# The running sum of an encoder layer's output: from SBUF with VectorE's adds to DRAM with accumulating transfers

## The chip, the cores and the metric

One core of one Trainium2 chip runs the kernel. The metric is the device time of one execution in microseconds (us), the median of several runs.

## What is computed

One encoder layer on x of 512 tokens by 2048 features, in float32. A mixing stage (two head groups, a gated unit and a long convolution) ends in a projection that is added to x. Then comes the feed-forward layer, which this case is about, and a last normalization:

```python
h = rms_norm(x, norm2_g[l])
gv = h @ ffn_w_up[l]                                  # 2048 -> 2 * 5504
g = dwconv3(gv[..., :D_FF], ffn_dw_w[l], ffn_dw_b[l]) # three taps along the tokens
val = gv[..., D_FF:]
x = x + (jax.nn.gelu(g, approximate=False) * val) @ ffn_w_down[l]
...
return rms_norm(x, final_g)
```

## The kernel before

Every large matmul works on pairs: a float32 operand is split into a high part that TensorE takes exactly and the rest, and three matmuls (line 222, `mm3`) make one product. For weights ScalarE casts the high part and VectorE subtracts it from the raw tile (`exact_pair`, lines 143 and 144). Raw tiles of 512 KB come in SP's order from a plan (lines 88 to 125): `raw` with three buffers for w_in, w_out and w_up, `sraw` with four for w_down; cast and subtract run up to three units ahead of TensorE (`next_unit`, line 203). A scheduler of the framework orders each engine's instructions; each engine and SP then run theirs strictly in that order.

The feed-forward layer runs over 11 groups of up to 512 of the 5504 inner features. A group has 8 units of the gate's projection and 8 of the value's (`regular`, 24 matmuls each), with ScalarE, VectorE and GpSimd convolving and gating between (`conv_piece`, whose multiply by GpSimd is line 1113; `value_out`; `operands`). The multiplication by w_down of groups 0 to 9 is done for blocks of two by two with seven products (`strassen`, units 0 to 6, for each of two halves `dp` of the output columns: 14 units of 12 matmuls a group). These units stand between the projection units of the group after (`ffn_order`, lines 95 to 107); for the last of the ten groups products 3 to 6 of the second half follow the last projection without others between. Product u runs into a chain of two PSUM banks (tp = 0 and 1); a chain is read out after each product that ends in it, and some are then added to further.

The running sum x lies in SBUF, in `xacc` (32 KB of each partition). At the start of the layer `turn_x` turns it so that tokens lie on the partitions. After each product `down_out` has VectorE add the two banks to their place in it (`add_to`, line 1192). Product 3 belongs to three blocks; it is summed over the groups in `shared` (line 1201) and added three times at the end. For `next_unit` such work waits in `posts`, for `piece` in `pieces`.

The 11th group (384 features) takes no products of that kind: its w_down comes in eight tiles of 512 or 256 KB (units "L"), and 144 matmuls make sixteen blocks of 128 tokens by 512 columns; `last_out` adds a block to x, squares it and multiplies it by final_g (`grow`), `leave` scales it and stores it. First come the blocks of tokens 0 to 255, tile by tile as the weights come, then the others. Lines 1253 to 1350 hold this end.

Of the kernel before, what the change touches and what calls it, by code (L numbers as in the profile page):

```python
# [12 lines left out]
F32 = mybir.dt.float32  # L13
F32R = mybir.dt.float32r
AF = mybir.ActivationFunctionType
ALU = mybir.AluOpType

P = 128
D = 2048
# [32 lines left out]
def encoder_kernel(ctx: ExitStack, tc: tile.TileContext, a: dict, out: bass.AP):  # L52
# [783 lines left out]
    kp = pool("keep", side="right", stack=keep)  # L836
    xacc = kp.tile([P, KD, L], F32, name="xacc")
    ds_ = ExitStack()
# [16 lines left out]
    def done_a(q, ps):  # L855
        for f, o in enumerate(ps):
            ACT.copy(xacc[:, 4 * q + f, :], o)

# [140 lines left out]
    def done_b(q, ps):  # L999
        ts_ = []  # L1000
        for f, o in enumerate(ps):
            t = bo.tile([P, L], F32, tag="ev", name="tb", bufs=4)
            DVE.tensor_tensor(t, o, rbs[0], ALU.mult)
            ts_.append(t)
        for f, t in enumerate(ts_):
            x_ = xacc[:, 4 * q + f, :]
            POOL.tensor_tensor(t, t, res[q][:, f, :], ALU.add)
            DVE.tensor_tensor(x_, x_, t, ALU.add)
# [9 lines left out]
    def norm2(q):  # L1018
        H, Lo = h2[q]
        if q == 0:  # L1020
            ss2s.append(const.tile([P, L], F32, tag="acc", name="ss2", bufs=1))
        ss2 = ss2s[0]
        for f in range(4):
            k = 4 * q + f
            split_scaled(H[:, f, :], Lo[:, f, :], xacc[:, k, :], col("norm2", k))
            sq = (bo if q < 3 else A3).tile([P, L], F32, tag="ev", name="sq2", bufs=4 if q < 3 else 2)
            square_into(ss2, xacc[:, k, :], sq, k == 0)

# [37 lines left out]

    shared = ff.tile([P, 2, 2, 512], F32, name="shared")
    special["raw"] = lambda: ff.tile([P, 2, 512], F32, tag="sraw", name="sraw", bufs=4)
# [15 lines left out]

    def out_tile(t, q):

        return xacc[:, 4 * q : 4 * q + 4, t * P : (t + 1) * P]

    def as_out(ap):
        return ap.rearrange("p (k c) -> p k c", k=4)  # L1090

    def turn_x(k):

        o = sbank("xt")
        for t in range(NT):
            PE.transpose(o[:, t * P : (t + 1) * P], xacc[:, k, t * P : (t + 1) * P], ident)
        ACT.copy(xacc[:, k, :], o)

# [16 lines left out]
    def gate_out(gi):  # L1115
        gg[gi] = ff.tile([P, 4, L], F32, tag="gg", name="gg", bufs=1)
        for f, o in enumerate(ps_of.pop(("gate", gi))):
            DVE.tensor_tensor(gg[gi][:, f, :], o, r2[0], ALU.mult)
            pieces.append(lambda f=f: conv_piece(gi, f))
# [69 lines left out]

    def add_to(t, q, src):  # L1190
        x_ = out_tile(t, q)
        DVE.tensor_tensor(x_, x_, src, ALU.add)

    def down_out(gi, dp, u, tp):
        o = chains[dp, CHAIN[u]][tp]
        if u == 3:
            sh = shared[:, tp, dp, :]
            if gi == 0:
                ACT.copy(sh, o)
            else:  # L1200
                DVE.tensor_tensor(sh, sh, o, ALU.add)
            if gi == last - 1:
                for t, q in ((tp, dp + 2), (tp + 2, dp), (tp + 2, dp + 2)):
                    pieces.append(lambda t=t, q=q: add_to(t, q, as_out(sh)))
        else:
            t, q = ((tp, dp), (tp + 2, dp + 2), (tp, dp + 2), None, (tp + 2, dp + 2), (tp, dp), (tp + 2, dp))[u]
            add_to(t, q, as_out(o))

    def strassen(e):
# [9 lines left out]
        for tp in range(2):  # L1219
            ts_ = slice(tp * P, (tp + 1) * P)  # L1220
            for k in range(2):
                mm3(
                    chains[dp, CHAIN[u]][tp], H[:, u, k, ts_], Lo[:, u, k, ts_], hi[:, k, :], lo[:, k, :],
                    k == 0 and u not in (2, 3, 6), k == 1, True,
                )
            posts.append(lambda tp=tp: down_out(gi, dp, u, tp))

# [44 lines left out]
    def last_operands():  # L1272
        g = gg.pop(last)
        for f in range(nf):
            exact_pair(aH[:, f, :], aL[:, f, :], g[:, f, :])
        grow.append(ff.tile([P, D], F32, tag="gg", name="grow", bufs=1))
        SP.dma_start(grow[0], a["final_g"].partition_broadcast(P))

    grow, fin = [], {}
    for e in units:  # L1280
        if e[0] == "L":
# [6 lines left out]
    def last_out(t, q):  # L1288

        if q == 0:  # L1290
            if t < 2:
                w = ff.tile([P, D], F32, tag=("aH", "aL")[t], name="fin", bufs=1)
                fin[t] = [w[:, i * 512 : (i + 1) * 512] for i in range(4)]
            else:
                ws = [special["raw"]() for _ in range(2)]
                fin[t] = [ws[i // 2][:, i % 2, :] for i in range(4)]
        o = ps_of.pop(("last", t, q))
        x_ = fin[t][q]
        DVE.tensor_tensor(as_out(x_), out_tile(t, q), as_out(o), ALU.add)
        ACT.activation(tmp[q % 2], x_, AF.Square, accum_out=ssf[:, t, q : q + 1])  # L1300
# [10 lines left out]
    def leave(t):  # L1311
# [12 lines left out]
        for q in (0, 1, 3, 2):  # L1324
            SP.dma_start(out[t * P : (t + 1) * P, q * 512 : (q + 1) * 512], fin[t][q])

    for q in range(4):
        for k0 in range(0, nf, 2):
# [105 lines left out]
```

## Time and profile before

| | us |
|---|---|
| median of 3 runs (2086.36 to 2088.26) | 2087.02 |
| the profiled execution, its own time | 2086.55 |
| its span in the profile | 2084.7 |
| TensorE (PE) busy | 2059.8 |
| VectorE (DVE) busy | 1374.5 |
| ScalarE (ACT) busy | 758.6 |
| GpSimd (POOL) busy | 215.4 |
| bytes moved by DMA, mean over the span | 228.33 MB, 110 GB/s |

Busy times of the engines lie beside each other, so they don't add up to the span. A matmul of 512 columns is listed with some 390 ns, but matmuls are pipelined and start closer together than that. An engine's idle time is listed with what ended it. SP and the other queues that issue transfers are not counted as busy; a transfer's time to landing is listed with its issue. The DMA share is the mean busy share of the core's 16 DMA engines.

### The profile page before, as it was taken

To read this page: it belongs to the slowest core of one execution; us is meant where nothing else is said; L and a number is where in the kernel's file an instruction comes from. 1 tells how busy PE (TensorE), PEld (TensorE's weight loads), DVE (VectorE), ACT (ScalarE), POOL (GpSimd) and SP (SyncE) were. 2 spreads that over 40 slices of the span, in tenths; PEclk is the share of its full clock that TensorE was granted. 3 is DMA by queue.
4 is the path that set the end of the run, shared out by engine and by line. 5 is a ranking of instruction groups with operands and counts; after the bars stand their busy time and mean duration, and the time that the engine had idled before them with its cause. 6 is when DMAs were issued, how large, how long until landed. Compare 5 with 4: busy or idle time off the path is not lost.

```text
span 2084.7 us, 23478 instructions
## 1 busy us (share of the span) xinstructions
PE 2059.8 (99%) x9374; PEld 1706.9 (82%) x9374; DVE 1374.5 (66%) x1654; ACT 758.6 (36%) x954; POOL 215.4 (10%) x124
## 2 busy tenths in 40 slices
PE   8999999999999999999999999999999999999997
PEld 6888887888888888888888888888888888888886
DVE  6873565556897944755757666676755757666768
ACT  6433542222544442332333332333322333332334
POOL 0330211000003610100101001010100101001000
PEclk9999999999999999999999999999999999999999
DMA  8434233243323532332333333333332333333223
GB/s 298 137 116 141 81 91 91 81 141 105 108 82 121 172 91 82 100 113 90 111 97 104 103 101 102 91 101 102 101 113 90 111 97 103 105 101 94 91 84 136
DMA packets 112697, 228.33 MB, mean 110 GB/s; under 512 B 7147, under 2 KB 14507, under 8 KB 110668
## 3 DMA queue, kind: packets, MB, share of 16 engines
q1 hardware_dynamic: 107248, 216.74, 33.3%
q10 hardware_dynamic: 5340, 10.10, 1.4%
q8 instruction: 73, 1.20, 0.2%
q14 instruction: 36, 0.29, 0.0%
HBM read 218.42 MB, written 8.39 MB: 109 GB/s over the span
## 4 chain that ended last, share of the span: by engine, by line
PE 90%; DVE 7%; ACT 1%; issue 1%; DMA 1%; POOL 0%; ACTq 0%; SPq 0%; POOLq 0%; DVEq 0%
PE pa L226 19%; PE pa L224 19%; PE pa L225 19%; PE po L224 2%; PE po L226 2%; PE po L225 2%; PE se L225 2%; PE se L226 2%; PE se L224 2%; PE sa L225 2%; PE sa L226 2%; PE sa L224 2%; PE sc L225 2%; PE sc L224 2%; PE sc L226 2%; PE pv L224 1%
## 5 line engine op out<-in xcount | busy, mean ns | idle before, releaser
L224 PE MATMUL pa<-h2H,hi 128*128 128x512 f32 x1376 | 536.7, 390 | 0.0
L144 DVE TENSOR_TENSOR lo<-raw,hi 128x1024 fp32r<-128x1024 f32 (+2 forms) x289 | 358.8, 1245 | 269.6 <-ACT hi L143 269.5
L226 PE MATMUL pa<-h2H,lo 128*128 128x512 f32 x1376 | 535.6, 389 | 0.0
L225 PE MATMUL pa<-h2L,hi 128*128 128x512 f32 x1376 | 535.4, 389 | 0.0
L143 ACT CAST hi<-raw 128x1024 fp32r<-128x1024 f32 (+2 forms) x289 | 299.2, 1036 | 536.3 <-PE pa L225 252.0
L144 DVE TENSOR_TENSOR lo<-sraw,hi 128x1024 fp32r<-128x1024 f32 x140 | 171.6, 1226 | 317.3 <-ACT hi L143 317.2
L143 ACT CAST hi<-sraw 128x1024 fp32r<-128x1024 f32 x140 | 147.5, 1054 | 468.5 <-PE pa L225 399.6
L226 PEld LDWEIGHTS pa<-h2H,lo 128*128 128x128 f32 x1376 | 258.3, 188 | 53.7
L225 PEld LDWEIGHTS pa<-h2L,hi 128*128 128x128 f32 x1376 | 258.4, 188 | 53.3
L224 PEld LDWEIGHTS pa<-h2H,hi 128*128 128x128 f32 x1376 | 258.4, 188 | 53.1
L1113 POOL TENSOR_TENSOR gg<-gg,r 128x512 f32<-128x512 f32 x43 | 90.7, 2121 | 1166.2 <-ACT gg L1112 1166.2
L224 PE MATMUL pa<-hH,hi 128*128 128x512 f32 x512 | 202.0, 395 | 2.4 <-DVE ev L615 1.5
L226 PE MATMUL pa<-hH,lo 128*128 128x512 f32 x512 | 200.1, 392 | 1.5 <-DVE lo L144 1.5
L225 PE MATMUL pa<-hL,hi 128*128 128x512 f32 x512 | 200.2, 391 | 0.0
L224 PEld LDWEIGHTS pa<-hH,hi 128*128 128x128 f32 x512 | 96.7, 189 | 28.1 <-DVE ev L615 4.5
L226 PEld LDWEIGHTS pa<-hH,lo 128*128 128x128 f32 x512 | 96.5, 189 | 23.4 <-DVE lo L144 3.0
L225 PEld LDWEIGHTS pa<-hL,hi 128*128 128x128 f32 x512 | 96.7, 189 | 19.1
L180 DVE TENSOR_TENSOR sraw<-sraw 128x1024 f32<-128x1024 f32 x80 | 98.7, 1234 | 18.3 <-DMA sraw<-in_ffn_w_down 18.0
L224 PE MATMUL sc<-hi,aH 128*128 128x512 f32 x160 | 62.3, 390 | 0.1
L226 PE MATMUL sc<-hi,aL 128*128 128x512 f32 x160 | 62.3, 389 | 0.0
L224 PE MATMUL sa<-hi,aH 128*128 128x512 f32 x160 | 62.2, 389 | 0.0
L225 PE MATMUL sa<-lo,aH 128*128 128x512 f32 x160 | 62.2, 389 | 0.0
(282 smaller groups left out, 3053.1 us busy)
## 6 DMA issues: line engine op xcount, KB each, us to landing
raw<-in_ffn_w_up SPq DMA_DIRECT2D x160, 512.0 KB, 3.7
sraw<-in_ffn_w_down SPq DMA_DIRECT2D x80, 512.0 KB, 3.8
raw<-in_w_in SPq DMA_DIRECT2D x79, 512.0 KB, 3.7
raw<-in_w_out SPq DMA_DIRECT2D x32, 512.0 KB, 3.7
raw<-in_ffn_w_up SPq DMA_DIRECT2D x16, 384.0 KB, 3.3
xn<-in_xN ACTq DMA_DIRECT2D x8, 512.0 KB, 4.7
khat_d<-kh SPq DMA_DIRECT2D x4, 1024.0 KB, 4.4
kh<-khat_d SPq DMA_DIRECT2D x4, 1024.0 KB, 4.8
```

The source lines that it names most:

```text
L143: ACT.copy(hi, src)
L144: eng.tensor_tensor(lo, src, f32(hi), ALU.subtract)
L180: DVE.tensor_tensor(raws[i], sraws[gi, dp, of], sraws[gi, dp, less], ALU.subtract)
L224: PE.matmul(o, ah, bh, start=start, stop=False, skip_group_check=read)
L225: PE.matmul(o, ah, bl, start=False, stop=False, skip_group_check=read)
L226: PE.matmul(o, al, bh, start=False, stop=stop, skip_group_check=read)
L1113: POOL.tensor_tensor(e, e, r2[0], ALU.mult)
```

## The change

The sum moves to a DRAM tile `xd`, in blocks [column quarter q, token block t, 128 tokens, 512 columns]. `xacc` becomes four tiles `xa` (tag with four buffers); after `turn_x` of the fourth part of a quarter SP stores that quarter with four transfers. The four buffers then serve `gg` (which had one) in turn, and at the end `fin`, the blocks of the final sum. `down_out` copies a product's two banks with ScalarE into a staging tile `cs` (three buffers, 512 KB) and GpSimd issues one accumulating transfer of it for each block that the product belongs to: one each, three for product 3. `shared` and all of VectorE's adds to `xacc` go. Before the last part SP loads the 16 blocks of the sum; `last_out` adds the bank to them. Transfers to the same block wait for each other, and a load of a block waits for its last add.

```diff
-    xacc = kp.tile([P, KD, L], F32, name="xacc")
+    xas = [kp.tile([P, 4, L], F32, tag="xa", name="xa", bufs=4) for _ in range(4)]
+
+    def xa(k):
+        return xas[k // 4][:, k % 4, :]
...
-    shared = ff.tile([P, 2, 2, 512], F32, name="shared")
+    xd = dram.tile([4, NT, P, 512], F32, name="xd")
...
     def turn_x(k):
 
         o = sbank("xt")
+        q, x_ = k // 4, xa(k)
         for t in range(NT):
-            PE.transpose(o[:, t * P : (t + 1) * P], xacc[:, k, t * P : (t + 1) * P], ident)
-        ACT.copy(xacc[:, k, :], o)
+            PE.transpose(o[:, t * P : (t + 1) * P], x_[:, t * P : (t + 1) * P], ident)
+        ACT.copy(x_, o)
+        if k % 4 == 3:
+            for t in range(NT):
+                SP.dma_start(
+                    xd[q, t].rearrange("p (k c) -> p k c", k=4), xas[q][:, :, t * P : (t + 1) * P]
+                )
...
-        gg[gi] = ff.tile([P, 4, L], F32, tag="gg", name="gg", bufs=1)
+        gg[gi] = kp.tile([P, 4, L], F32, tag="xa", name="gg", bufs=4)
...
-    def add_to(t, q, src):
-        x_ = out_tile(t, q)
-        DVE.tensor_tensor(x_, x_, src, ALU.add)
-
-    def down_out(gi, dp, u, tp):
-        o = chains[dp, CHAIN[u]][tp]
-        if u == 3:
-            sh = shared[:, tp, dp, :]
-            if gi == 0:
-                ACT.copy(sh, o)
-            else:
-                DVE.tensor_tensor(sh, sh, o, ALU.add)
-            if gi == last - 1:
-                for t, q in ((tp, dp + 2), (tp + 2, dp), (tp + 2, dp + 2)):
-                    pieces.append(lambda t=t, q=q: add_to(t, q, as_out(sh)))
-        else:
-            t, q = ((tp, dp), (tp + 2, dp + 2), (tp, dp + 2), None, (tp + 2, dp + 2), (tp, dp), (tp + 2, dp))[u]
-            add_to(t, q, as_out(o))
+    OUTS = ([(0, 0)], [(1, 1)], [(0, 1)], [(0, 1), (1, 0), (1, 1)], [(1, 1)], [(0, 0)], [(1, 0)])
+
+    def down_out(dp, u):
+
+        st = ff.tile([P, 2, 512], F32, tag="cs", name="cs", bufs=3)
+        for tp in range(2):
+            ACT.copy(st[:, tp, :], chains[dp, CHAIN[u]][tp])
+        for th, dh in OUTS[u]:
+            dst = xd[dp + 2 * dh, 2 * th : 2 * th + 2].rearrange("t p c -> p t c")
+            POOL.dma_start(dst, st, accum_op=ALU.add)
...
-            posts.append(lambda tp=tp: down_out(gi, dp, u, tp))
+        posts.append(lambda: down_out(dp, u))
...
+    def load_fin(t):
+        w = kp.tile([P, 4, L], F32, tag="xa", name="fin", bufs=4)
+        fin[t] = [w[:, q, :] for q in range(4)]
+        for q in range(4):
+            SP.dma_start(fin[t][q], xd[q, t])
...
-        DVE.tensor_tensor(as_out(x_), out_tile(t, q), as_out(o), ALU.add)
+        DVE.tensor_tensor(x_, x_, o, ALU.add)
...
+    flush()
+    for t in range(NT):
+        load_fin(t)
     for q in range(4):
         for k0 in range(0, nf, 2):
             next_unit(("L", k0, q), flush)
```

Where the order of the instructions moves, by engine (a name's number is that of its buffer; `x2` stands for two equal ones):

On SP at the end of the kernel, before: from `grow` (final_g) to the first stores of the output; the `raw` tiles are the last five of the eight w_down tiles of the 11th group.

```order
L1277 DMA grow_14408<-in_final_g 128x2048
L139 DMA raw_14455<-in_ffn_w_down 128x512
L139 DMA raw_14476<-in_ffn_w_down 128x2x512
L139 DMA raw_14494<-in_ffn_w_down 128x512
L139 DMA raw_14512<-in_ffn_w_down 128x2x512
L139 DMA raw_14528<-in_ffn_w_down 128x512
L1325 DMA out_0<-fin_14484 128x512 x4
```

With the change, on SP from the sixth of the eight tiles on; `fin_14783`, `fin_14788`, `fin_14793` and `fin_14798` are the sum's blocks of tokens 0, 128, 256 and 384.

```order
L139 DMA raw_14839<-in_ffn_w_down 128x512
L139 DMA raw_14857<-in_ffn_w_down 128x2x512
L1280 DMA fin_14783<-xd_5597 128x512
L1280 DMA fin_14788<-xd_5597 128x512
L1280 DMA fin_14793<-xd_5597 128x512
L1280 DMA fin_14798<-xd_5597 128x512
L1280 DMA fin_14793<-xd_5597 128x512
L1280 DMA fin_14798<-xd_5597 128x512
L139 DMA raw_14873<-in_ffn_w_down 128x512
L1320 DMA out_0<-fin_14783 128x512 x4
```

Six loads of the sum now stand ahead of the eighth tile, `raw_14873`, the fifth of them (of tokens 256, column quarter 1) bound to the add of product 6. Ten others stand further ahead, between the tiles.

On GpSimd after the last group's gating, before; line 289 is the root of the final normalization, line 1113 the multiply of the gate.

```order
L1113 TENSOR_TENSOR gg_12418<-gg_12418,r2_5854 128x512 x4
L1113 TENSOR_TENSOR gg_13247<-gg_13247,r2_5854 128x512 x4
L1113 TENSOR_TENSOR gg_14030<-gg_14030,r2_5854 128x512 x3
L289 TENSOR_TENSOR r3_14612<-r3_14612,nhalf_106 128x1
L289 TENSOR_TENSOR r3_14650<-r3_14650,nhalf_106 128x1
L289 TENSOR_TENSOR r3_14690<-r3_14690,nhalf_106 128x1
```

With the change, on GpSimd in the same place, from product 6 of the first half on (line 1116 is the multiply of the gate, `cs` the staging tile of a product):

```order
L1202 DMA xd_5597<-cs_14403 128x2x512
L1116 TENSOR_TENSOR gg_14346<-gg_14346,r2_5865 128x512
L1202 DMA xd_5597<-cs_14459 128x2x512
L1202 DMA xd_5597<-cs_14505 128x2x512
L1202 DMA xd_5597<-cs_14551 128x2x512
L1202 DMA xd_5597<-cs_14705 128x2x512 x3
L1202 DMA xd_5597<-cs_14759 128x2x512
L1202 DMA xd_5597<-cs_14739 128x2x512
L1202 DMA xd_5597<-cs_14779 128x2x512
L289 TENSOR_TENSOR r3_14955<-r3_14955,nhalf_106 128x1
```

Where GpSimd had nothing to do it now issues the adds of products 6 (first half) and 0, 1, 2, 3, 5, 4, 6 (second half); product 3 (`cs_14705`) has three, and product 5's (`cs_14759`) stands ahead of product 4's (`cs_14739`).

On ScalarE in the last products, before: `hi` are casts for products, `lH` and `laH` those of the 11th group's weights and gated activations.

```order
L143 CAST hi_14303<-sraw_14138 128x1024
L143 CAST hi_14326<-sraw_14038 128x1024
L143 CAST hi_14363<-sraw_14330 128x1024
L143 CAST laH_14357<-gg_14030 128x512 x3
L143 CAST lH_14355<-raw_14388 128x2x512
L143 CAST lH_14355<-raw_14417 128x512
L143 CAST lH_14355<-raw_14436 128x2x512
L143 CAST hi_14384<-sraw_14330 128x1024
L143 CAST lH_14355<-raw_14455 128x512
```

With the change, on ScalarE in the same place, from the cast for product 6 on:

```order
L143 CAST hi_14711<-sraw_14653 128x1024
L1199 COPY cs_14739<-sc_14702 128x512
L1199 COPY cs_14739<-sc_14703 128x512
L143 CAST lH_14678<-raw_14745 128x512
L143 CAST lH_14678<-raw_14765 128x2x512
L1199 COPY cs_14759<-sg_14737 128x512
L1199 COPY cs_14759<-sg_14738 128x512
L143 CAST lH_14678<-raw_14805 128x512
L1199 COPY cs_14779<-sc_14702 128x512
L1199 COPY cs_14779<-sc_14703 128x512
```

Each product's two copies stand among the casts of the last weight tiles; those of product 6 (`cs_14779`) come behind the cast of the fourth tile (`raw_14805`).

## Rows read from the trace of the kernel before

**Rows 1.** The page, part 1: busy us of each engine, share, instructions.

```profile
PE 2059.8 (99%) x9374; PEld 1706.9 (82%) x9374; DVE 1374.5 (66%) x1654; ACT 758.6 (36%) x954; POOL 215.4 (10%) x124
```

**Rows 2.** Busy time of each engine by stretches of the span.

```profile
core 0: us, PE busy (x) PEld busy (x) DVE busy (x) ACT busy (x) POOL busy (x), PEclk, DMA share, GB/s
0.00:100.00 100.00, 91.54 (x424) 72.78 (x425) 74.56 (x98) 57.67 (x79) 19.17 (x13) 1.00 0.63 219
1000.00:1400.00 400.00, 400.00 (x1766) 331.31 (x1766) 264.89 (x302) 131.12 (x145) 33.25 (x16) 1.00 0.33 100
2020.00:2040.00 20.00, 19.87 (x88) 16.15 (x88) 13.88 (x18) 8.10 (x10) 0.00 (x0) 1.00 0.21 79
2040.00:2060.00 20.00, 19.66 (x86) 15.53 (x85) 19.51 (x31) 8.62 (x19) 0.00 (x0) 1.00 0.30 93
2070.00:2085.00 15.00, 4.59 (x21) 3.46 (x19) 6.43 (x15) 5.04 (x12) 1.45 (x2) 0.78 0.50 181
```

**Rows 3.** Timeline of GpSimd: start, us, engine, line, out<-in, idle before.

```profile
997.87 2.17 POOL L1113 TENSOR_TENSOR gg<-gg,r 128x512 f32<-128x512 f32 x1 [111.11 <-ACT gg L1112]
...
1122.98 2.17 POOL L1113 TENSOR_TENSOR gg<-gg,r 128x512 f32<-128x512 f32 x1 [111.10 <-ACT gg L1112]
```

**Rows 4.** Busy time over one group of the feed-forward layer.

```profile
1000.00:1122.00 122.00, 122.00 (x540) 101.02 (x540) 78.73 (x91) 37.95 (x42) 6.71 (x4) 1.00 0.32 100
```

**Rows 5.** VectorE in line 1192, then in 1201, over the span; the group of line 857.

```profile
0.00:2085.00 2085.00, 167.91 (x252) 1.00 0.35 110
...
0.00:2085.00 2085.00, 24.53 (x36) 1.00 0.35 110
...
L857 ACT COPY xacc<-po 128x512 f32<-128x512 f32 x16 | 9.4, 588 | 11.0 <-PE po L226 10.2
```

**Rows 6.** Timeline of one group: SP's issues, VectorE, ScalarE, TensorE.

```profile
1104.40 0.37 SPq L157 DMA_DIRECT2D sraw<-in_ffn_w_down  x1
...
1107.30 0.37 SPq L139 DMA_DIRECT2D raw<-in_ffn_w_up  x1
...
1104.29 1.36 DVE L1201 TENSOR_TENSOR shared<-shared,sa 128x512 f32<-128x512 f32 x2
...
1108.34 1.23 DVE L180 TENSOR_TENSOR sraw<-sraw 128x1024 f32<-128x1024 f32 x1 [1.07 <-DMA sraw<-in_ffn_w_down]
...
1111.26 1.23 DVE L144 TENSOR_TENSOR lo<-sraw,hi 128x1024 fp32r<-128x1024 f32 x1 [1.70 <-ACT hi L143]
...
1119.78 1.22 DVE L144 TENSOR_TENSOR lo<-raw,hi 128x1024 fp32r<-128x1024 f32 x1
...
1133.01 1.04 ACT L143 CAST hi<-raw 128x1024 fp32r<-128x1024 f32 x1
...
1118.36 0.39 PE L224 MATMUL sg<-hi,aH 128*128 128x512 f32 x1
...
1123.80 0.39 PE L224 MATMUL pa<-h2H,hi 128*128 128x512 f32 x1
```

**Rows 7.** DMA issues: KB each and median us to landing.

```profile
raw<-in_ffn_w_up SPq DMA_DIRECT2D x160, 512.0 KB, 3.7
...
raw<-in_ffn_w_down SPq DMA_DIRECT2D x4, 256.0 KB, 3.3
```

**Rows 8.** Timeline of the end: TensorE, SP, ScalarE, VectorE.

```profile
2032.05 0.39 PE L226 MATMUL sa<-hi,aL 128*128 128x512 f32 x1
...
2041.07 0.39 PE L226 MATMUL sc<-hi,aL 128*128 128x512 f32 x1
...
2074.20 0.39 PE L226 MATMUL pl<-lH,laL 128*128 128x512 f32 x1
...
2050.15 0.33 SPq L139 DMA_DIRECT2D raw<-in_ffn_w_down  x1
...
2053.78 0.60 ACT L143 CAST lH<-raw 128x512 fp32r<-128x512 f32 x1
...
2055.65 0.68 DVE L144 TENSOR_TENSOR lL<-raw,lH 128x512 fp32r<-128x512 f32 x1
```

More of the change, by code (lines that the diff above doesn't have):

```diff
@@ L856, in done_a @@
         for f, o in enumerate(ps):
-            ACT.copy(xacc[:, 4 * q + f, :], o)
+            ACT.copy(xa(4 * q + f), o)
     def quad(tag):
@@ L1005, in done_b @@
         for f, t in enumerate(ts_):
-            x_ = xacc[:, 4 * q + f, :]
+            x_ = xa(4 * q + f)
             POOL.tensor_tensor(t, t, res[q][:, f, :], ALU.add)
@@ L1024, in norm2 @@
             k = 4 * q + f
-            split_scaled(H[:, f, :], Lo[:, f, :], xacc[:, k, :], col("norm2", k))
+            split_scaled(H[:, f, :], Lo[:, f, :], xa(k), col("norm2", k))
             sq = (bo if q < 3 else A3).tile([P, L], F32, tag="ev", name="sq2", bufs=4 if q < 3 else 2)
-            square_into(ss2, xacc[:, k, :], sq, k == 0)
+            square_into(ss2, xa(k), sq, k == 0)
     ybk = lambda k: yb[k]
@@ L1083, in hk @@
         return H[:, k % 4, :], Lo[:, k % 4, :]
[L1085 to L1090, printed above, removed]
     def turn_x(k):
         o = sbank("xt")
+        q, x_ = k // 4, xa(k)
         for t in range(NT):
-            PE.transpose(o[:, t * P : (t + 1) * P], xacc[:, k, t * P : (t + 1) * P], ident)
-        ACT.copy(xacc[:, k, :], o)
+            PE.transpose(o[:, t * P : (t + 1) * P], x_[:, t * P : (t + 1) * P], ident)
[5 more added lines that the diff above has]
+                )
     ps_of = {}
@@ L1275, in last_operands @@
             exact_pair(aH[:, f, :], aL[:, f, :], g[:, f, :])
-        grow.append(ff.tile([P, D], F32, tag="gg", name="grow", bufs=1))
+        grow.append(lp_.tile([P, D], F32, name="grow"))
         SP.dma_start(grow[0], a["final_g"].partition_broadcast(P))
     grow, fin = [], {}
+    def load_fin(t):
[3 more added lines that the diff above has]
+            SP.dma_start(fin[t][q], xd[q, t])
     for e in units:
@@ L1288, in last_out @@
     def last_out(t, q):
[L1290 to L1296, printed above, removed]
         o = ps_of.pop(("last", t, q))
         x_ = fin[t][q]
-        DVE.tensor_tensor(as_out(x_), out_tile(t, q), as_out(o), ALU.add)
+        DVE.tensor_tensor(x_, x_, o, ALU.add)
         ACT.activation(tmp[q % 2], x_, AF.Square, accum_out=ssf[:, t, q : q + 1])
```

## The prediction, made before the changed kernel was run

> **What bounds the kernel now.** I read the page's busy times first. TensorE is busy 2059.8 us of the span of 2084.7 [rows 1], so all its idle time together is 24.9 us, and a change that leaves its matmuls alone can win no more than a part of that. The busy time by stages says which part. The first 100 us hold 8.5 us of idle time that the change doesn't touch; in the stage of the feed-forward layer TensorE is busy 400 of 400 us, one 128x512 matmul every 400/1766 = 0.2265 us; the 40 us around the last products lose 0.13 + 0.34 us; the last 15 us lose 10.4, after the last matmul [rows 2]. In the same 400 us VectorE is busy 265 us, ScalarE 131 and GpSimd 33, and the granted clock is 1.00 throughout, the upper level of 2.4 GHz [rows 2]. So VectorE, which the change relieves, isn't what TensorE waits for.
>
> One group of the layer takes 1122.98 - 997.87 = 125.1 us by GpSimd's first multiply in two groups that follow each other [rows 3]. In it lie 24 loads of 512 KB (16 of w_up, 8 of w_down), which keep the DMA engines busy for 0.32 of the time [rows 4]: 40 us in 125.1, or 1.67 us of all 16 engines for each load.
>
> **The change, part by part.**
>
> *VectorE's adds go.* 252 adds of line 1192 (167.9 us) and 36 of line 1201 (24.5 us) [rows 5]. They lie beside matmuls; worth 0 in the steady stage.
>
> *ScalarE's copies come.* 280 copies of a bank, at 588 ns as in line 857 [rows 5]: 165 us, 28 in a group, 16.5 us on top of some 41 (131/400 x 125.1). ScalarE stays under half. Behind a pair of copies (1.2 us) the casts of weights wait. The tightest pair I found has VectorE end its part of a tile at 1119.78 + 1.22 = 1121.0 and TensorE start on it at 1123.80 [rows 6]; there the cast stands ahead of the copies. Cost 0, up to a delay of 2.8 us.
>
> *Stores and loads on SP.* 16 stores of 256 KB when the sum is turned, and 16 loads of 256 KB at the end. The weight loads queued behind them have cover: one issued at 1107.30 is cast three casts of its kind later, at 1133.01, though a load needs 3.7 us [rows 6, 7]. The tightest, issued at 1104.40, is used by VectorE at 1108.34 after a wait of 1.07 us; behind it the tile cast and ready at 1111.26 + 1.23 = 1112.5 is needed at 1118.36 [rows 6], so another 5.9 us of lateness costs nothing. 0 in the steady stage; the end is taken below.
>
> *The accumulating transfers* are the one large new thing: 180, that is 18 of 512 KB in a group, one for each 6.95 us, all from GpSimd. The trace has none, so I bound the engine time of one: as a plain load, 1.67 us, from below; as three transfers of its size (source read, old sum read, new sum written), 5.0 us, from above. With 18 in a group the engines' share becomes 0.56, or 1.04. I take 2, that is 3.3 us (share 0.80): a load too reads and writes, and the add puts one more read to that; of the two ends this is nearer to the load, the only row there is. The Trainium skill (Collectives: The Full Stack, section "The bandwidth ceiling: the fold count and why AG ≠ RS ≠ AR") says that an adding transfer reads two sources and measures it at 62.28/32.35 = 1.93 times a copy; by that an add here would be 3.2 us, an estimate that no run here shows yet. As latency I add what a load has beyond its engine time, 3.7 - 1.67 = 2.0 us [rows 7]. GpSimd's cost of issuing one has no row; between nothing and one multiply of 2.17 us [rows 3]. Three together (product 3) are then out 1.2 + 10 + 2 = 13.2 us after the product's end; their staging tile is wanted again by product 6, and TensorE wants that product's copies only after it: from the end of product 3 (1104.29, where VectorE could start on its banks) to the end of product 6 (1123.80) there are 19.5 us [rows 6]. So in the steady stage the adds are hidden: 0.
>
> *The end* is where they show. The last products 3, 4, 5 and 6 follow each other without other matmuls between. Product 4's add on block (1,1) waits for product 3's third add; product 6's add stands behind product 4's in GpSimd's order; two loads of the finished sum wait for product 6's add; and SP issues the last weight tile behind those two. Before, that tile waited for its buffer alone and was issued at 2050.15 [rows 8]. The chain now: product 3's last matmul starts at 2032.05 and takes 0.39 [rows 8]; a copy of 0.59 [rows 5], with casts about it, ends by 2033.3. Three adds and one latency, 3 x 3.3 + 2.0: 2045.2. Two adds and one latency, 2 x 3.3 + 2.0: 2053.8. The load of 256 KB 3.3 [rows 7], the cast 0.60 and the subtract 0.68 [rows 8]: 2058.4. TensorE wants that tile after 66 of the 144 matmuls of the last layer part. All of these now come behind product 6; it ended before with a matmul started at 2041.07 [rows 8], ahead of which two of the 144 had gone, so the first of the 144 starts at 2041.07 + 0.23 - 0.45 = 2040.85 and the 67th at 2055.8. So 2.6 us late.
>
> To that comes the traffic. In those 20 us SP asks for 3 MB of other loads (six of 256 KB for the sum, two of 512 and two of 256 KB of weights), 6 x 1.67 = 10 us of engine time; none to all of it may lie ahead of the chain. I take half, 5: 7.6 us late.
>
> Against that, without any lateness the last matmul would start at 2040.85 + 143 x 0.2265 = 2073.2 and not at 2074.20 [rows 8]: a gain of 1.0, from a VectorE that no longer adds there. What follows the last matmul keeps its length.
>
> *Sum:* 2086.55 (the profiled execution, 1.85 over its span) + 7.6 - 1.0 = 2093.2. The median of the runs, 2087.02, is 0.5 higher, less than I can resolve.
>
> *Bounds.* With 1.67 us an add, product 3's are in by 2040.3, product 6's copies (its end at 2041.0, two of 0.59) at 2042.2 set the pace, its add is in by 2045.9 and the tile ready at 2050.5, 5.3 us early: no loss, 2085.5. With 5.0: 2050.3, 2062.3, 2066.9, that is 11.1 late, with all the other loads 21.1, less 1.0: 2106.7.
>
> **The rivals.**
>
> *The end is hidden too.* The tile is early as long as an add takes less than 2.8 us of engine time without other traffic (2033.3 + 5 adds + two latencies + 4.6 below 2055.8), or 1.8 with half of it. For it: the DMA engines stand at 0.30 in the stretch of the end [rows 2], and a cheap add falls near a load. Against: two adds in a row behind three, with one weight load after them. Time 2085.5 to 2091.2.
>
> *The engines fill up.* An add that holds the engines over (125.1 - 40)/18 = 4.7 us can't be done 18 times in a group. Then the three staging tiles stay taken, ScalarE waits to copy, and its casts and TensorE behind it. At 5.0 a group needs 130.2 us; ten groups add 51, the end 20: 2156, and each further 0.1 us of an add costs 18 more. Against: it takes three full transfers for one add.
>
> *Faster by more than a measurement tells.* It would need over 4.2 of the 24.9 us of idle time, while only 0.5 us in the stretch of the end [rows 2] and the 1.0 above can be reached. I see no place for it.
>
> **How the numbers follow.** About 0.2% (4.2 us around 2087.02, so 2082.8 to 2091.2) is what a measurement tells from no change. A late end 0.58, a hidden one 0.29, full engines 0.10, faster 0.03. Slower by over 0.2% is the first and the third, 0.68; within it 0.29; faster 0.03. The range takes the first two cases with their bounds, 2085.5 to 2106.7, and leaves out the full engines and the faster case, 0.13.
>
> **What would show it.** Right: TensorE at 400 of 400 us in the steady stage, a share of the DMA engines there near 0.8, and one wait of some microseconds before a matmul of the last part, led back through the cast of a w_down tile to SP, which waited for the sum's loads and they for an accumulating transfer. Time from issue to landing of one add near 5.3 us. Wrong: no such wait, and the last matmul near 2073 (hidden); or idle TensorE in each group with ScalarE waiting for a transfer to free a staging tile (full); or a loss at the place where the sum is turned and stored, which I put at 0.

## The result and the profile after

| | us |
|---|---|
| the kernel before, median of 4 runs (2086.36 to 2088.26) | 2086.69 |
| the changed kernel, median of 4 runs (2099.64 to 2101.48) | 2099.89 |
| ratio, with its 95% interval | 1.0063 (1.0046 to 1.0081) |
| forecast, range | 2093.2, 2085.5 to 2106.7 |

The change is 13.2 us slower; 6.2 were forecast. The profiled execution of the change has a span of 2099.7 us, 15.0 more than that of before; it is the slowest of the four, 1.6 above their median. The page's busy times:

```profile
PE 2065.5 (98%) x9374; PEld 1711.0 (81%) x9374; DVE 1218.8 (58%) x1366; ACT 898.3 (43%) x1230; POOL 406.7 (19%) x304
```

VectorE has lost 155.7 us of work against [rows 1], ScalarE has got 139.7, and GpSimd, whose issues of adds are listed as busy time, 191 more. TensorE has the same 9374 matmuls and is busy 5.7 us longer. Where, the busy times by stretches tell (columns as in [rows 2]):

```profile
1000.00:1400.00 400.00, 400.00 (x1766) 331.20 (x1766) 216.44 (x208) 177.24 (x238) 92.39 (x74) 1.00 0.80 178
2020.00:2040.00 20.00, 20.00 (x89) 16.54 (x89) 13.00 (x15) 10.75 (x16) 3.65 (x3) 1.00 0.40 104
2040.00:2050.00 10.00, 10.00 (x46) 8.28 (x45) 1.31 (x2) 0.96 (x2) 1.19 (x1) 1.00 1.05 243
2050.00:2055.00 5.00, 0.59 (x3) 0.17 (x1) 0.00 (x0) 1.41 (x3) 2.40 (x2) 0.83 1.09 284
2055.00:2060.00 5.00, 3.78 (x8) 2.69 (x9) 3.02 (x4) 2.83 (x5) 0.00 (x0) 0.50 1.10 255
2065.00:2070.00 5.00, 0.82 (x3) 0.19 (x1) 2.37 (x4) 1.34 (x3) 0.00 (x0) 1.00 0.49 159
2070.00:2075.00 5.00, 4.80 (x14) 3.85 (x15) 4.55 (x9) 2.80 (x8) 0.00 (x0) 0.66 0.00 0
```

In the steady stage TensorE does 1766 matmuls in 400 of 400 us, to the matmul as before, though the DMA engines now stand at 0.80 instead of 0.33. All of the loss is in the last 60 us: the DMA engines are full from 2040 on (1.05 to 1.10; the share can pass 1, of which more below), TensorE is all but idle in 2050 to 2055 and in 2065 to 2070, and after each of the two gaps the granted clock is down for some microseconds (0.50, the lower level of 1.2 GHz, in 2055 to 2060). The timeline of TensorE, from the last matmul of product 6 to the last of all, with its waits:

```profile
2042.04 0.39 PE L226 MATMUL sc<-hi,aL 128*128 128x512 f32 x1
...
2055.76 0.80 PE L224 MATMUL pl<-lH,laH 128*128 128x512 f32 x1 [5.17 <-ACT lH L143]
2057.01 0.80 PE L225 MATMUL pl<-lL,laH 128*128 128x512 f32 x1 [0.46 <-DVE lL L144]
...
2069.48 0.49 PE L224 MATMUL pl<-lH,laH 128*128 128x512 f32 x1 [4.15 <-ACT lH L143]
2070.20 0.71 PE L225 MATMUL pl<-lL,laH 128*128 128x512 f32 x1 [0.23 <-DVE lL L144]
...
2089.15 0.39 PE L226 MATMUL pl<-lH,laL 128*128 128x512 f32 x1
```

The 144 matmuls of the last part run from 2042.27 (a step of 0.2265 behind product 6) to 2089.15, 46.9 us. Unhindered they need 143 x 0.2265 = 32.4. The waits are 5.17 + 0.46 + 4.15 + 0.23 = 10.0; the 4.5 us that remain are matmuls at the lower clock behind the waits. Between the same two matmuls lie 47.1 us now and 33.1 before [rows 8]: 14.0 of the two executions' difference of 15.0 (the other 1.0 lies ahead of the end, and in the runs below with four staging tiles and with six more adds product 6 ends 1.9 and 1.3 us earlier than here, so it isn't the change's). What follows the last matmul takes 10.5 us in both.

What the two waits hang on, from the timelines of SP, GpSimd, ScalarE and VectorE:

```profile
2042.45 5.43 SPq L139 DMA_DIRECT2D raw<-in_ffn_w_down  x3
2054.94 10.41 SPq L1280 DMA_DIRECT2D fin<-xd  x6
2065.45 0.38 SPq L139 DMA_DIRECT2D raw<-in_ffn_w_down  x1
...
2035.24 3.65 POOL L1202 DMA_DIRECT2D xd<-cs  x3 [21.97 <-ACT cs L1199]
...
2051.15 2.43 POOL L1202 DMA_DIRECT2D xd<-cs  x2 [9.32 <-DMA xd<-cs]
...
2051.01 1.07 ACT L1199 COPY cs<-sc 128x512 f32<-128x512 f32 x2 [4.26 <-DMA xd<-cs]
2054.66 1.04 ACT L143 CAST lH<-raw 128x1024 fp32r<-128x1024 f32 x1 [2.58 <-DMA raw<-in_ffn_w_down]
...
2068.81 0.62 ACT L143 CAST lH<-raw 128x512 fp32r<-128x512 f32 x1 [2.46 <-DMA raw<-in_ffn_w_down]
...
2069.46 0.69 DVE L144 TENSOR_TENSOR lL<-raw,lH 128x512 fp32r<-128x512 f32 x1 [2.38 <-ACT lH L143]
```

The second wait is the forecast one: product 3's three adds issued from 2035.24, products 4 and 6 on GpSimd waiting for them until 2051.15, the sum's six loads on SP from 2054.94 (when product 5's add, issued at 2040.64, lands) to 2065.35, and behind them the eighth weight tile, issued at 2065.45 and cast at 2068.81. The first wait was not forecast: it is for the fifth tile (512 KB), issued at 2042.45, ahead of those six loads and no later than before (at 2042.53 there), and not landed before 2054.66. The DMA issues of 2041 to 2044 show it among adds that take as long (KB each, us to landing):

```profile
xd<-cs POOLq DMA_DIRECT2D x1, 512.0 KB, 14.3
...
raw<-in_ffn_w_down SPq DMA_DIRECT2D x1, 512.0 KB, 12.2
```

A tile that lands 3.7 us after its issue elsewhere [rows 7] took 12.2 here, between adds that took 14.3.

### The profile page after: what moved, and what is told of

Its sections match the earlier page's. It is cut to its first block, busy times and chain, and to the rows that moved or that the text cites. A ratio compares the mean times of both kernels' runs of the same rounds, so it can differ in the third digit from the quotient of the medians.

```text
span 2099.7 us, 23963 instructions
## 1 busy us (share of the span) xinstructions
PE 2065.5 (98%) x9374; PEld 1711.0 (81%) x9374; DVE 1218.8 (58%) x1366; ACT 898.3 (43%) x1230; POOL 406.7 (19%) x304
## 4 chain that ended last, share of the span: by engine, by line
PE 89%; DVE 6%; DMA 2%; ACT 1%; issue 1%; POOL 0%; SPq 0%; ACTq 0%; POOLq 0%; DVEq 0%
PE pa L224 19%; PE pa L226 19%; PE pa L225 19%; PE po L225 2%; PE po L224 2%; PE po L226 2%; PE se L226 2%; PE se L224 2%; PE se L225 2%; PE sa L226 2%; PE sa L224 2%; PE sa L225 2%; PE sc L226 2%; PE sc L225 2%; PE sc L224 2%; PE pv L224 1%
## 5 line engine op out<-in xcount | busy, mean ns | idle before, releaser
L1202 POOL DMA_DIRECT2D xd<-cs x180 | 224.6, 1414 | 959.5 <-ACT cs L1199 797.4
L144 DVE TENSOR_TENSOR lo<-sraw,hi 128x1024 fp32r<-128x1024 f32 x140 | 199.0, 1421 | 332.3 <-ACT hi L143 332.2
L1116 POOL TENSOR_TENSOR gg<-gg,r 128x512 f32<-128x512 f32 x43 | 71.6, 1832 | 65.5 <-ACT gg L1115 65.5
L1199 ACT COPY cs<-se 128x512 f32<-128x512 f32 x80 | 47.1, 589 | 51.5 <-PE se L226 51.5
```

What stands on the lines that cost most here:

```text
L144: eng.tensor_tensor(lo, src, f32(hi), ALU.subtract)
L1116: POOL.tensor_tensor(e, e, r2[0], ALU.mult)
L1199: ACT.copy(st[:, tp, :], chains[dp, CHAIN[u]][tp])
L1202: POOL.dma_start(dst, st, accum_op=ALU.add)
```

## The experiments

**Theory.** The loss lies in the end alone and comes from the last half group's adds and the sum's loads there, by two ways: *order* (SP can't issue the eighth tile before loads that wait for adds) and *traffic* (the adds and loads fill the DMA engines, and tiles that stand behind nothing land late). **Rivals**: staging tiles; the price of an add; the steady stage near its limit; the copies and stores.

### Order: the sum's loads on another queue

```diff
-            SP.dma_start(fin[t][q], xd[q, t])
+            POOL.dma_start(fin[t][q], xd[q, t])
```

> Only the 16 loads of the finished sum go from SP's queue to GpSimd's; nine of them then stand behind product 6's add, and no weight tile waits behind them on SP. Theory (order on SP): the 4.4 us wait for the last weight tile and the slow clock behind it go, about 5.5 us: 2094. If the first wait (5.6 us, for the fifth tile) comes from the sum's loads that share the DMA engines with the weights, it goes too: 2086 to 2089. Rival (the wait turns to VectorE): the sum's blocks of column quarter 1 now come later, VectorE's add of them stands ahead of its subtract for the last weight tiles, and TensorE waits there instead: 2096 or more.

Measured: 2095.87 us (before in these runs 2086.99; ratio 1.0042, 1.0027 to 1.0056), 4.0 less than the change. TensorE's waits in the last part and its last matmul, and a wait of VectorE:

```profile
2051.29 0.51 PE L224 MATMUL pl<-lH,laH 128*128 128x512 f32 x1 [2.48 <-ACT lH L143]
2052.55 0.51 PE L225 MATMUL pl<-lL,laH 128*128 128x512 f32 x1 [0.76 <-DVE lL L144]
...
2078.34 0.39 PE L226 MATMUL pl<-lH,laL 128*128 128x512 f32 x1
...
2060.19 0.69 DVE L144 TENSOR_TENSOR lL<-raw,lH 128x512 fp32r<-128x512 f32 x1 [2.58 <-ACT lH L143]
```

The wait for the eighth tile is gone, and the first is 3.2 instead of 5.6. It hangs on something else now: the fifth tile, asked for before 2038, lands after 10.4 us, by 2048.4, but its cast on ScalarE stands behind product 6's copies, which get their staging tile from product 3's adds at 2049.22 only. From product 6 to the last matmul 38.1 us pass instead of 47.1, but behind that matmul 15.6 instead of 10.5 (span 2093.9): at 2061.4 VectorE still has 14 of the 16 blocks to do. No wait of VectorE for a block of the sum is listed here; its last long one is for the cast of the eighth tile, until 2060.19, and the loads of the sum issued from 2054.58 on took 6.4 us, so that they landed at about the same time. Which of the two held it this run doesn't tell. So 9 us are won on TensorE and 5 given back on VectorE. The time, 0.1 below the rival's bound, lies where the rival put it, but TensorE doesn't wait for VectorE in the place that the rival named; the loss shows behind the last matmul.

### Staging tiles

```diff
-        st = ff.tile([P, 2, 512], F32, tag="cs", name="cs", bufs=3)
+        st = ff.tile([P, 2, 512], F32, tag="cs", name="cs", bufs=4)
```

> Only the staging tiles go from three to four. In the changed kernel ScalarE waited 4.3 us for a staging tile before product 6's copies, and cast weights behind them. Theory (order on SP, traffic): the tile that TensorE waited for first had not landed by then, and product 6's add waits behind product 4's on GpSimd in any case: the same within 1.5 us, 2098.5 to 2101. Rival (staging): product 6's add comes out some 2 to 4 us earlier and with it the sum's last loads and the last weight tile: 2095 to 2097.

Measured: 2099.94 us (1.0063, 1.0048 to 1.0078): the same. ScalarE's timeline shows product 6's copies without a wait, at 2044.93 and not at 2051.01, and the cast behind them waiting for a tile to land:

```profile
2044.93 1.06 ACT L1199 COPY cs<-sc 128x512 f32<-128x512 f32 x2
2052.76 1.57 ACT L143 CAST lH<-raw 128x1024 fp32r<-128x1024 f32 x2 [6.76 <-DMA raw<-in_ffn_w_down]
```

A wait was taken away that another one covered.

### The price of an add

```diff
-            POOL.dma_start(dst, st, accum_op=ALU.add)
+            POOL.dma_start(dst, st)
```

> The same transfers write instead of adding, so the running sum is left out. Theory (an add costs twice a plain transfer, and the end is late by the adds): engine time of one falls from 3.4 to about 1.7 us, the share of the DMA engines in the steady stage from 0.80 to about 0.56, both waits in the end shrink to 0 to 2 us together: 2086.5 to 2090. Rival (the length of the queues and waits, not the price of an add): the end keeps over half of its loss: 2094 or more.

Measured: 2091.03 us (1.0019, 1.0010 to 1.0029), 8.9 less than the change and 4.0 more than before. GpSimd's queue in 1000 to 1400 us (packets, MB, share of 16 engines), first in the change, then here:

```profile
q0 software_dynamic: 16037, 30.92, 49.3%
```

```profile
q0 software_dynamic: 8223, 29.91, 21.4%
...
xd<-cs POOLq DMA_DIRECT2D x58, 512.0 KB, 4.2
```

With 58 transfers in either stretch that is 0.493 x 400/58 = 3.40 us of all engines for an add and 1.48 for a write. (An add also goes out in about twice as many packets for the same bytes.) The end got shorter, but even at 1.48 the fifth tile makes TensorE wait (1.2 + 0.8 us), and what follows the last matmul takes 12.1 us, 1.6 more than before: the time lies between theory and rival, nearer to the theory. TensorE's two waits:

```profile
2049.62 0.50 PE L224 MATMUL pl<-lH,laH 128*128 128x512 f32 x1 [1.19 <-ACT lH L143]
...
2050.88 0.80 PE L225 MATMUL pl<-lL,laH 128*128 128x512 f32 x1 [0.76 <-DVE lL L144]
```

### How much the steady stage still takes

Some products are sent out a second time, to blocks `xe` of their own; here products 0, 5 and 6, in the second run all:

```diff
             POOL.dma_start(dst, st, accum_op=ALU.add)
+            if gi < last - 1 and u in (0, 5, 6):
+                xt = xe[dp + 2 * dh, 2 * th : 2 * th + 2].rearrange("t p c -> p t c")
+                POOL.dma_start(xt, st, **({'accum_op': ALU.add} if gi else {}))
```

> In nine of the ten groups each of six products is sent out a second time, to a block of its own: 24 transfers in a group and not 18. Theory (the steady stage hides all that the engines can do in 125.1 us): 40 + 24 x 3.4 = 121.6 us, a share of 0.97, TensorE still without waits in the steady stage: 2098 to 2105. Rival (the steady stage was close to its limit, by staging tiles or the weights' lateness): over 10 us lost for each of the groups: 2190 or more. Between: 3 to 8 us a group, 2125 to 2170.

> In nine of ten groups every transfer is sent out a second time, to a block of its own (plain in the first group, adding from the second on): 36 adds in a group. Theory (engines full): 38 + 36 x 3.2 to 3.4 = 153 to 160 us of engine time in a group of 125.1, 28 to 35 us lost in each of eight groups: 2320 to 2400; share of the DMA engines near 1.0 or above, TensorE waiting for casts, ScalarE for staging tiles. Rival (the engines take more at a time than that sum says): 2110 to 2200. Rival (the adds on one block wait for each other and the queue breaks down): 2450 or more.

Measured with 24 transfers in a group: 2100.35 us (1.0063, 1.0048 to 1.0078), as the change with 18. Its queue in 1000 to 1400 us, with 78 transfers there:

```profile
q0 software_dynamic: 21663, 41.78, 61.4%
```

Measured with 36: 2164.36 us (1.0366, 1.0352 to 1.0381), 64 more. This one's stretch from 1000 to 1400 us, its queue, and a wait of ScalarE in it (us in total, times, longest):

```profile
1000.00:1400.00 400.00, 384.92 (x1660) 316.20 (x1660) 201.93 (x195) 164.64 (x219) 151.53 (x120) 0.97 1.09 237
```

```profile
q0 software_dynamic: 29430, 56.72, 79.8%
```

```profile
ACT cs L1200 <- DMA xe<-cs: 28.9, 4, 8.6
```

Of each kind 54 transfers (three groups' worth) were issued in these 400 us, so a group takes 133 us instead of 125.1: the engines are full, ScalarE waits for staging tiles and TensorE for casts, as the theory has it, but only 8 us are lost in a group, where it said 28 to 35. The engine time of one transfer is 0.798 x 400/108 = 2.96 us there, and 0.614 x 400/78 = 3.15 with 24. So the first rival of the second run came true (2110 to 2200): full engines take more than a sum of prices from the change's stage says. 18 and 24 adds in a group cost nothing; 36 are over the limit.

### The last half kept in SBUF

The sum's blocks of column quarters 1 and 3 are loaded before the last seven products, which VectorE adds to them; the fourth token block's two quarters have a tile of their own.

```diff
+        if (gi, dp) == (last - 1, 1):
+            for tp in range(2):
+                for th, dh in OUTS[u]:
+                    x_ = fin[tp + 2 * th][dp + 2 * dh]
+                    DVE.tensor_tensor(x_, x_, chains[dp, CHAIN[u]][tp], ALU.add)
+            return
...
+            if e == ("S", last - 1, 1, 0):
+                flush()
+                load_fin(1)
```

> The sum stays in DRAM for everything but the last half of the last group: those blocks are loaded before it, and VectorE adds its seven products to them in SBUF, so that no adding transfer runs in the last 40 us and no load waits for one. Theory (the loss comes from the adds and loads of the last half alone; copies, spills and the 171 other adds cost nothing): from the end of product 6 to the last matmul about 33 us as in the kernel before (47 in the change), 2085.5 to 2087.5. Rival (the copies, the stores of the sum or VectorE's and ScalarE's order keep a part of it): 2089 or more.

Measured: 2088.05 us, with 2087.75 before in these runs: ratio 1.0003 (0.9995 to 1.0012). That is 0.55 above the theory's range, but the kernel before took 1.1 more in these runs than in the first ones. 171 adds, the 16 stores, the 16 loads and 266 of ScalarE's 280 copies stay, and no loss can be told from the kernel before. One wait is new, as TensorE's timeline shows; product 3's six adds stand in a row on VectorE ahead of a bank that product 6 needs:

```profile
2041.63 0.47 PE L224 MATMUL sc<-hi,aH 128*128 128x512 f32 x1 [1.86 <-DVE fin L1201]
```

Then the traffic alone was put back: the same copies and adds, to blocks that nobody reads.

```diff
+            st = ff.tile([P, 2, 512], F32, tag="cs", name="cs", bufs=3)
+            for tp in range(2):
+                ACT.copy(st[:, tp, :], chains[dp, CHAIN[u]][tp])
+            for th, dh in OUTS[u]:
+                POOL.dma_start(xe[dp + 2 * dh, 2 * th : 2 * th + 2].rearrange("t p c -> p t c"), st, accum_op=ALU.add)
             return
```

> As the kernel with the last half in SBUF, but the last half's copies and adding transfers are issued as in the change, to blocks that nobody reads: their traffic without their waits. (In the first group too the second half is written there a second time.) Theory A (traffic: the weight tiles land late because the adds hold the DMA engines): the weight tiles of the last part take 8 us or more to land and TensorE waits 2 to 6 us, with a slow clock behind it: 2089 to 2094. Theory B (order: only the loads that wait for the adds and the tile behind them cost): within 1.5 us of the kernel without that traffic, 2085.5 to 2088.5.

Measured: 2097.43 us (1.0048, 1.0032 to 1.0063), 9.4 more than without. Two of TensorE's waits, and GpSimd's last issues:

```profile
2054.23 0.65 PE L224 MATMUL pl<-lH,laH 128*128 128x512 f32 x1 [1.70 <-ACT lH L143]
...
2066.10 0.50 PE L225 MATMUL pl<-lL,laH 128*128 128x512 f32 x1 [0.82 <-DVE lL L144]
...
2037.19 3.65 POOL L1207 DMA_DIRECT2D xe<-cs  x3 [19.92 <-ACT cs L1205]
2052.49 3.66 POOL L1207 DMA_DIRECT2D xe<-cs  x3 [11.65 <-issue]
```

No load of the sum waits for an add here, and weight tiles still come late: the fourth, asked for at 2041.60, is cast at 2049.70. Order can't be the whole (theory B falls). The size lies above theory A's range, and not all of it is traffic: the waits for weight tiles are 3.9 us in all, and another 2.1, in the place of the 1.9 above, are for copies that wait behind VectorE on the same banks, which is this edit's own. The traffic isn't quite that of the change either: the last three adds go out together from 2052.49, where the change issues product 5's at 2040.64 and the other two from 2051.15. So 9.4 is the price of this traffic in this kernel, and no clean figure for its part in the change.

### Weight tiles early

Weight tiles 4 to 7 get the four w_down buffers, and all eight are asked for earlier; the program order puts them ahead of the sum's loads that wait.

```diff
-            raws[i] = load_raw((w_dn, groups[last][0] + k0, min(2, groups[last][1] - k0), q * 512, 512))
+            raws[i] = load_raw(
+                (w_dn, groups[last][0] + k0, min(2, groups[last][1] - k0), q * 512, 512),
+                special["raw"]() if 3 <= 2 * q + k0 // 2 < 7 else None,
+            )
...
-        dma_to(i + 4)
+        dma_to(i + (11 if plan[i][0] == "S" and plan[i][1:3] == (last - 1, 1) and plan[i][3] > 2 else 4))
```

> The change with all its transfers; only the last part's weight tiles 4 to 7 are loaded into the four w_down buffers that the last products give free, and all eight tiles are asked for earlier, ahead of the loads of the sum that wait. Theory (traffic and order both act through weight tiles that come late): the tiles are asked for by 2040 and land, at some 8 us each, before TensorE wants them (2050 for the fifth, 2057 for the eighth); both waits go, and what is left is the sum's blocks that come late to VectorE at the end, 2 to 5 us as in the run with the loads on GpSimd: 2088.5 to 2092. Rival (the traffic itself can't be moved: the same bytes in the same stretch still make a tile or the sum late): 2094 or more.

Measured: 2094.28 us (1.0037, 1.0024 to 1.0050). TensorE's only wait of the last part and its last matmul, and VectorE's wait for the sum:

```profile
2050.57 0.50 PE L227 MATMUL pl<-lH,laH 128*128 128x512 f32 x1 [1.10 <-ACT cs L1202]
...
2074.28 0.39 PE L229 MATMUL pl<-lH,laL 128*128 128x512 f32 x1
...
2059.98 1.50 DVE L1297 TENSOR_TENSOR fin<-fin,pl 128x512 f32<-128x512 f32 x2 [2.81 <-DMA fin<-xd]
```

The wait left to TensorE is for the cast behind product 6's copies and their staging tile, as with the loads on GpSimd. TensorE ends where it ended before (2074.20 [rows 8]), and the kernel is still 7.6 us slower than before: behind the last matmul lie 18.3 us. So there is a second deadline. Product 5's add was issued at 2039.27 and landed 14.1 us later, the load of its block took 7.0, and from 2060 on VectorE and ScalarE have 14 of the 16 blocks to add, square, scale and send off. That is the rival in its strong form: the same traffic makes the sum late when it doesn't make the weights late.

The last part then took the column quarters in the order 0, 2, 1, 3 (0 and 2 belong to products long finished), in the second run with four staging tiles as well:

```diff
-    for q in range(4):
+    for q in (0, 2, 1, 3):
...
-        for q in range(4):
+        for n, q in enumerate((0, 2, 1, 3)):
```

> As the kernel with the early weight tiles, and the last part takes the column quarters in the order 0, 2, 1, 3: quarters 0 and 2 belong to the first half of the products, whose sums are long finished. Theory (what is left is the sum's arrival: product 5's add lands at 2053.4, its block's load at 2060.7, and from then VectorE and ScalarE have 14 blocks to do, which end 18 us behind the last matmul): when the late blocks are wanted, four blocks are done and not two, so 2 x 1.45 = 2.9 us go: 2090.5 to 2092. Rival (VectorE's start is set by something else, such as ScalarE's 10 us wait for a staging tile with three casts behind it): 2093.5 to 2095.

> As the kernel before it with four staging tiles: ScalarE's 10 us wait before product 6's copies goes, and the casts of the last three weight tiles come some 6 us earlier. Theory (the sum's arrival ends last): the same as with three, within 1 us. Rival (staging): now that the weight tiles are early, the wait for a staging tile is what VectorE's subtracts and the blocks behind them hang on: 1.5 us or more faster than with three.

Measured: 2092.17 us (1.0025, 1.0015 to 1.0035) and 2091.57 us (1.0024, 1.0014 to 1.0033). The first is 0.2 over its theory's range, the two are the same within 1 us, though the fourth staging tile takes TensorE's wait away (2.0 us in the first). In the second TensorE has no wait left, while VectorE, with the four blocks done that don't need a late sum, waits for the sum:

```profile
2059.00 1.38 DVE L1297 TENSOR_TENSOR fin<-fin,pl 128x512 f32<-128x512 f32 x2 [1.65 <-DMA fin<-xd]
...
2072.47 0.39 PE L229 MATMUL pl<-lH,laL 128*128 128x512 f32 x1
```

Behind its last matmul 16.1 us pass (span 2088.6): the sum's arrival ends last. With every wait of TensorE gone, the sum's way through DRAM still costs 5 us.

### A version without the loss

The edit against the kernel with the last half in SBUF, in part; `late` keeps product 3's adds for the last part, where they are taken two at a time.

```diff
-                    DVE.tensor_tensor(x_, x_, chains[dp, CHAIN[u]][tp], ALU.add)
+                    if u == 3:
+                        late.append(lambda tp=tp, th=th, dh=dh: add(tp, th, dh, st[:, tp, :]))
+                    else:
+                        add(tp, th, dh, src)
```

> The kernel with the last half in SBUF, with product 3's six adds of that half taken from a copy that ScalarE makes, in the last part, and not in one row behind the product. In the run before TensorE waited 1.9 us for VectorE's add on a bank that product 6 needed. Theory: that wait goes and 1 to 2 us with it: 2085.5 to 2087, at best 0.1% faster than the kernel before. Rival (VectorE's backlog in the last part grows by six adds, 4 us, and shows behind the last matmul): 2088 to 2091.

Measured: 2085.47 us, with 2086.72 before in these runs: ratio 0.9996 (0.9987 to 1.0005), so not told apart from the kernel before, and 14 us faster than the change. TensorE's last matmul:

```profile
2073.03 0.39 PE L226 MATMUL pl<-lH,laL 128*128 128x512 f32 x1
```

No wait is listed in the last part; 32.7 us pass between product 6 and this matmul, and 10.6 behind it.

## Why the prediction was right, and where it fell short

**Direction and place: right.** "Slower by over 0.2%, by a late end" had 0.58, and that is what came. The hidden end, the full engines and the gain did not.

**The steady stage at 0: right, and shown.** TensorE is busy 400 of 400 us. The forecast share of the DMA engines was 0.80, and 0.80 was measured; an add was put at 3.3 us of engine time and took 3.40. That copies, stores and 171 adds cost nothing is shown by the kernel that keeps them and changes the last half alone (1.0003). GpSimd's cost of issuing one was bounded by 0 and 2.17; single issues took 1.20. The Trainium skill (Collectives: The Full Stack, section "The bandwidth ceiling: the fold count and why AG ≠ RS ≠ AR") has an adding transfer, which reads two sources, at 1.93 times a copy; here an add took 3.40/1.48 = 2.30 times a plain write of the same size. The Trainium skill's figure sets ReduceScatter against AllGather in a ring of four ranks; for this add it is too low, and the measurement decides. One sign failed: an add was to land some 5.3 us after its issue, and in the steady stage (1000 to 1400 us) it took 7.9 in the median and 5.8 at the least, which cost TensorE nothing there.

**The end: the chain was right, each of its links was slower.** It was to be: product 3's adds in by 2045.2, product 6's by 2053.8, the eighth tile ready at 2058.4 and, with half of the other traffic, 2063.4. In the profile products 4 and 6 could be issued at 2051.15, SP had its last loads out at 2065.35, and the tile was ready at 2069.46 + 0.69 = 2070.15, 6.7 us later. Of these 6.7, 1.8 lie ahead of the chain: product 3's last matmul itself started 1.8 later in this execution (2033.88, and 2032.05 [rows 8]).

**The step that failed** is "I take half, 5: 7.6 us late", the size of the term for traffic. The 67th of the 144 matmuls, the first to need the eighth tile, would start unhindered at 2042.27 + 66 x 0.2265 = 2057.2. It starts at 2069.48, 12.3 us late and not 7.6. Less the 2.6 that the chain was to be late without other traffic, 9.7 are left for the term: nearly all of the 10 us of other loads, of which the prediction took half. That the two agree so well may be chance, for the delay doesn't come about as a queue ahead of one chain. In the profile the engines are full for 20 us, and whatever is asked for in that stretch comes late: an add after 14.3 us instead of 5.3, a 512 KB tile after 12.2 instead of 3.7.

So the fifth tile, which SP asks for as early as before and which the prediction didn't look at, makes TensorE wait too, and first (5.6 us). Beside the eighth it seems to add nothing: no link in the rows of the eighth tile's chain (GpSimd's adds, SP's loads, the tile, its cast) waits for TensorE, so without the first wait TensorE would have come to the second that much earlier, and 12.3 us late all the same. No run shows that alone; the run with the loads on GpSimd shows the reverse, the fifth tile late without the eighth, and TensorE needs 38.1 us there. Behind the eighth tile another 2.2 us are lost (14.5 up to the last matmul), 0.2 of them a wait for VectorE and the rest matmuls at the lower granted clock, for which the sum had no term.

The same step spoilt the lower bound, which left out all other traffic. At 1.67 us an add the eighth tile was to be 5.3 us early and the loss 0; plain writes took 1.48, and 4.0 us were lost, by the fifth tile and behind the last matmul.

**The split between order and traffic** is not settled. Taking the sum's loads off SP's queue gave back 4.0 us, and that is what is left after 5 of 9 us were lost again behind the last matmul. Traffic without SP's order cost 9.4, in a kernel with a wait of its edit's own and with some of the adds at other times. That the two add up to 13.4, near the 13.2 measured, proves nothing. Shown is that order alone isn't the loss, and that SP's order has a part in it.

**The gain of 1.0** from a VectorE that no longer adds in the end stays open. TensorE's last matmul was to start at 2073.2 without lateness, and in the version without the loss it starts at 2073.03. But there VectorE does add the last half's products in the end, so it doesn't test the reason; and the last matmul of product 6 starts anywhere between 2039.8 and 2042.0 in the kernels that keep the change's adds, so the time of a single one says little. From product 6 to the last matmul that version takes 32.7 us, the kernel before 33.1.

**The rivals' prices.** The engines were to be full at 4.7 us an add, 18 times a group; an add took 3.40, so that case didn't arise. The reasoning adds up engine times as if they were fixed. With 24 adds a group nothing was lost, and with 36 a group lost 8 us where 28 to 35 were expected from such a sum.

## What to carry to other kernels

A transfer that is free in the steady stage is paid where the work ends: look for the last stretch in which its result must be back, add up everything that is asked of the DMA engines there, and expect all of it to come late, not only the chain that you happen to follow. Here the chain was later by nearly all of the other loads' engine time (9.7 of 10 us), where half had been taken; one case makes that a first estimate and no rule. When a tail loses to traffic, moving one load out of the way hands the wait to the next consumer (here from the eighth weight tile to a staging tile, then to VectorE); what helped was to keep the last contributions out of DRAM altogether. And a wait of TensorE can cost more than its length, since the matmuls after it may run at the lower clock (some 2 us behind the wait for the eighth tile).

## What the runs showed that was not expected

**An add's engine time falls as the engines fill.** 3.40 us at 18 a group (share 0.80), 3.15 at 24 (0.92), 2.96 at 36 (1.09). So the mean busy share doesn't say how much is left: it passes 1, and at 0.80 the engines moved 178 GB/s, three quarters of the 237 that they moved at 1.09, with more adds beside each load.

**The sum's old values don't appear in the memory traffic.** The page's line on it, before and then in the change:

```profile
HBM read 218.42 MB, written 8.39 MB: 109 GB/s over the span
```

```profile
HBM read 222.61 MB, written 106.95 MB: 157 GB/s over the span
```

Read are 4.19 MB more, which is the 16 loads of 0.26 MB; written are 98.6 more, which is the 180 adds of 0.52 and the 16 stores. The kernel with plain writes shows the same two numbers. So the higher price of an add can't be read from these counters. It shows in the engine time (3.40 against 1.48) and in the packets (16037 against 8223); how much of it is the reading of the old values no run shows.

**The lower clock after short waits.** The granted clock fell to 0.50 not only behind the wait of 5.17 us: in the kernel with the last half in SBUF, behind 1.86 us of waiting, seven matmuls in a row start 0.43 us apart instead of 0.23, two of them here:

```profile
2043.44 0.63 PE L224 MATMUL sc<-hi,aH 128*128 128x512 f32 x1
2043.87 0.63 PE L225 MATMUL sc<-lo,aH 128*128 128x512 f32 x1
```

With plain writes it fell behind the waits of 1.19 and 0.76 us that follow closely on each other (0.50 in 2051 to 2053). Behind the one of 1.10 us in the kernel with the early tiles it stayed at 1.00 (2049 to 2056).
